# One pair of start addresses for all split weights of the up projection

## The chip, the cores and the metric

The kernel runs on one core of one Trainium2 chip. The metric is the device time of one execution in microseconds (us), and the time of a kernel is the median over several executions.

## The reference, cut to what matters

The program is one layer of a decoder trunk on a sequence of 256 tokens with 2048 channels, all in float32. A token mixer (sparse attention beside a matrix memory) comes first, a channel mixer follows. The change lies in the first matrix product of the channel mixer:

```
def conv_ffn(h, w_up, conv_w, conv_b, w_down):
    a, g = jnp.split(h @ w_up, 2, axis=-1)      # h: 256 x 2048, w_up: 2048 x 11264
    a = causal_dwconv(a, conv_w, conv_b)        # width 3
    return (jax.nn.silu(a) * g) @ w_down        # w_down: 5632 x 2048
```

`h @ w_up` is the "up projection", the product with `w_down` the "down projection".

## The kernel before, in words

**Split operands.** TensorE multiplies here in the format fp32r, which keeps fewer bits than float32. So every operand is split into a high part (rounded) and a low part (what the rounding left), and each product is made of three matmuls: high by high, high by low, low by high. A weight tile `w` of 128 partitions by 1024 float32 numbers (512 KB) comes by one DMA from the SP queue. ScalarE (ACT) casts it to `wh` (line 122), VectorE (DVE) subtracts to get `wl` (line 123). Both go into buffers that are 64 numbers wider than the tile, so that the tile may begin at any of several places in its buffer:

```
wh = wp.tile([P, 1024 + OFFN], F32R, name="wh", tag="wh", bufs=WB[1])[:, off:off + 1024]
wl = wp.tile([P, 1024 + OFFN], F32R, name="wl", tag="wl", bufs=WB[2])
wl = wl[:, offl:offl + 1024]
```

There are four buffers for `wh` and four for `wl`, used in turn. A buffer has (1024 + 64) x 4 = 4352 bytes in each partition, which is 17 x 256, and in the built program each of the eight begins at a multiple of 256 bytes. So the place in the buffer is also the place within 256 bytes: place 16 is byte 64, place 48 is byte 192.

**The up projection.** It is done in 44 blocks, `up(j)` for j = 0 to 43. Each block computes 128 channels of `a` and 128 channels of the gate for all 256 tokens, from four weight tiles of eight 128x128 pieces each. The weights are the stationary operand, and the activations `h2T` (high and low, 256 columns each, already in SBUF, every piece at a multiple of 1024 bytes from a start that is a multiple of 256) are the moving operand. For each piece stand three matmuls of 256 columns (line 93, by way of `mm_b`):

```
mm(ps, a, xt[:, k, 0, :], start, False)     # a: high part of the weights
mm(ps, a, xt[:, k, 1, :], False, False)
mm(ps, b, xt[:, k, 0, :], False, stop)      # b: low part
```

So a block has 4 x 8 x 3 = 96 matmuls, all with a weight load of 128x128 of their own, and writes one PSUM bank, `ps_up`. Afterwards ScalarE and VectorE do convolution, SiLU and gate from that bank while the next block runs.

**The places before.** The table `PLACES` has 22 pairs (place of the high part, place of the low part). Block j of the first half (j = 0 to 21) uses pair j, block j of the second half (22 to 43) uses pair 43 - j. So each pair serves two blocks, in reverse order, and neighbouring blocks nearly always have different pairs.

**What stands around the blocks.** Blocks 0 to 21 come right after the normalisation that makes `h2T` piece by piece; block 0 starts while TensorE still transposes the last pieces (line 1025). From block 3 on, a ticker (`tk.tick`) weaves the loads and products of one more adaptive row (`ada_rows`, lines 186 and 219) into the first half: DVE products, and two groups of eight TensorE transposes called `ps_adar`. Then the first half of the down projection runs (`proj_rows`, tile `ps_d`, 512 columns a matmul at first, 256 columns at the end), then blocks 22 to 43, then the second half of the down projection. Earlier in the program the input projection `ps_b` uses the same three matmuls with weights at one fixed pair of places, (16, 16).

Of the kernel before, what the change touches and what calls it, by code (L numbers as in the profile page):

```python
# [23 lines left out]
KF = DFF // P  # L24
# [14 lines left out]
NU0, NU1 = 4, 1  # L39
WARM = 20  # L40
OFFB, OFFA, OFFN = 16, 48, 64
PLACES = ((16, 16), (0, 0), (8, 8), (24, 24), (32, 32), (40, 40), (48, 48), (56, 56), (16, 16), (4, 4),
          (12, 12), (16, 48), (48, 16), (0, 16), (16, 0), (32, 0), (0, 32), (20, 20), (32, 48), (48, 32),
          (8, 40), (16, 16))
MORD = (0, 2, 1, 3)
PTV = 2
YA = 2
# [10 lines left out]
def build(ctx: ExitStack, tc: tile.TileContext, d, out, dbg=None):  # L58
# [36 lines left out]
    def t2(shape, name, dt=F32):  # L95
        return p0.tile(shape, dt, name=name, tag="t2", bufs=NT2)

    def bank(pool, name, dt=F32):
        return pool.tile([P, 512], dt, name=name, tag="b")

    def load(src):
        n = src.shape[-1]
        t = wp.tile([P, 1024], F32, name="w", tag="w", bufs=WB[0])
        nc.sync.dma_start(t[:, :n], src)
        return t
# [8 lines left out]
    def load_split(src, off=0, offl=None):  # L114

        n = src.shape[-1]
        t = load(src)
        wh = wp.tile([P, 1024 + OFFN], F32R, name="wh", tag="wh", bufs=WB[1])[:, off:off + 1024]
        wl = wp.tile([P, 1024 + OFFN], F32R, name="wl", tag="wl", bufs=WB[2])
        offl = off if offl is None else offl  # L120
        wl = wl[:, offl:offl + 1024]
        nc.scalar.copy(wh[:, :n], t[:, :n])  # L122
        lows.append(nc.vector.tensor_sub(wl[:, :n], t[:, :n], wh[:, :n]))  # L123
        return wh, wl
# [5 lines left out]
    def mm_b(ps, wh, wl, i, xt, k, start, stop):  # L130
        a, b = wh[:, i * P:(i + 1) * P], wl[:, i * P:(i + 1) * P]
        mm(ps, a, xt[:, k, 0, :], start, False)
        mm(ps, a, xt[:, k, 1, :], False, False)
        mm(ps, b, xt[:, k, 0, :], False, stop)
# [375 lines left out]
    for gi, kn in enumerate(GROUPS):  # L510
# [14 lines left out]
        for b in range(NBLK):  # L525
            if b % 2 == 0:
                ps = bank(psm, "ps_b")
            for k in range(k0, k0 + kn):
                wh, wl = next(wb)
# [14 lines left out]
        for c in range(6):  # L544
            pss = [bank(psm, "ps_a%d" % t) for t in range(2)]
            aw = AW if c < 4 else 512
            for k in range(k0, k0 + kn):
                wh, wl = next(wa if c < 4 else wv)
# [542 lines left out]
    KH = KF // 2  # L1091
# [8 lines left out]
    def up(j):  # L1100

        ps = bank(psm, "ps_up")
        for b in range(2):
            for hf in range(2):
                wh, wl = load_split(d["w_up"][j * 4 + b * 2 + hf], *PLACES[j if j < KH else KF - 1 - j])
                for k in range(8):
                    mm_b(ps[:, b * S:(b + 1) * S], wh, wl, k, h2T, hf * 8 + k, hf == 0 and k == 0,
                         hf == 1 and k == 7)
                tk.tick(UR)
        a, gate = ps[:, :S], ps[:, S:]  # L1110
        fw = lambda i: ffn[:, 3 * j + i:3 * j + i + 1]
        av = t2([P, S], "av")
        nc.scalar.activation(av, a, AF.Identity, bias=ffn[:, R_FB + j:R_FB + j + 1], scale=fw(2))
        for i in (1, 0):
            sh = 2 - i
            nc.vector.scalar_tensor_tensor(av[:, sh:], a[:, :S - sh], fw(i), av[:, sh:],
                                           op0=ALU.mult, op1=ALU.add)
        nc.scalar.activation(av, av, AF.Silu)
        nc.vector.tensor_mul(av, av, gate)
        u = uTt[:, j % KH]  # L1120
        nc.scalar.copy(u[:, 0, :], av)
        nc.vector.tensor_sub(u[:, 1, :], av, u[:, 0, :])

    for j in range(KH):
        up(j)
        if j == 2:
            for c in range(2):
                tk.add(ada_rows(5, g2, c))
# [3 lines left out]
    for j in range(KH, KF):  # L1132
        up(j)
# [147 lines left out]
```

## Time and profile before

| what | value |
|---|---|
| median of 3 runs | 1490.48 us |
| lowest and highest run | 1487.12 and 1491.28 us |
| the profiled execution: its time as the profile has it, the span from first to last instruction | 1488.3 us |
| granted TensorE clock, mean over the span | 0.984 |
| TensorE matmuls busy | 1439.8 us, 97% of the span |
| VectorE busy | 1071.9 us, 72% |
| ScalarE busy | 709.8 us, 48% |
| chain that ended last: `ps_up` matmuls | 33% of the span |
| blocks 0 to 21, and 22 to 43, from first to last matmul | 731.8 to 986.3 us, and 1108.1 to 1356.2 us |

The page gives no time of the profiled execution besides its span; the span is 2.2 us below the median of the runs shown. A matmul is recorded from its issue to its modelled end, so neighbours overlap, and the time that one costs is read from the distance of starts, or from a stretch divided by its count. In a view of stretches ("windows") for one tile, the count after PE is of all matmuls that overlap the stretch: a block of 96 shows 96 plus the two or three that are still ending, or beginning, at its edges.

### The profile page before, as it was taken

The page shows a single profiled execution, that of the slowest core. Times are in us where ns is not written, and L with a number is a line of the kernel's source. Part 1 is how long each engine was busy: PE and PEld are TensorE (multiplying, and loading weights), DVE is VectorE, ACT ScalarE, POOL GpSimd, SP SyncE. Part 2 cuts the span into 40 slices and gives each one's busy share as a digit, 9 for nine tenths or more (in the row PEclk, how much of TensorE's full clock was granted, in tenths as well). Part 3 has the DMA queues.
Part 4 walks back from the last instruction along what each step waited for, and adds up shares of the span by engine and source line. Part 5 has one row for each costly group of instructions (what it writes and reads, how often), then busy time and mean ns, then how long its engine had stood idle before and what let it go on. Part 6 is the DMA issues. An engine that isn't in the chain of part 4 may idle for free.

```text
span 1488.3 us, 24079 instructions
## 1 busy us (share of the span) xinstructions
PE 1439.8 (97%) x9470; PEld 1301.9 (87%) x9470; DVE 1071.9 (72%) x1565; ACT 709.8 (48%) x954; POOL 2.1 (0%) x6
## 2 busy tenths in 40 slices
PE   5999999999999999999699999999999999999997
PEld 4998998877667888888599999998899999999886
DVE  7899887888677898689867767755555555555566
ACT  5654443637664444435554444443334444444341
POOL 0000000000000000000000000000000000000000
PEclk8999999999999999999899999999999999999998
DMA  9999897885767999999078878866665555655661
GB/s 359 346 351 353 312 325 265 314 317 181 269 236 273 329 316 324 331 343 335 28 251 277 287 232 282 275 196 195 193 203 187 184 186 191 189 185 186 196 210 59
DMA packets 104081, 374.81 MB, mean 252 GB/s; under 512 B 11680, under 2 KB 12192, under 8 KB 103200
## 3 DMA queue, kind: packets, MB, share of 16 engines
q1 hardware_dynamic: 103968, 373.27, 72.9%
q8 instruction: 74, 1.21, 0.3%
q14 instruction: 39, 0.32, 0.1%
HBM read 371.13 MB, written 2.10 MB: 251 GB/s over the span
## 4 chain that ended last, share of the span: by engine, by line
PE 86%; DVE 7%; ACT 2%; DMA 2%; issue 2%; SPq 0%; DVEq 0%; ACTq 0%
PE ps_up L93 33%; PE ps_d L93 16%; PE ps_mg L93 11%; PE ps_b L93 7%; PE ps_br L93 6%; PE ps_o L93 5%; PE ps_a L93 5%; DVE w L186 2%; DVE wl L123 2%; DMA w<-in_w_in_b_dram 1%; PE ps_y L93 1%; ACT wh L122 1%; DVE xz L955 1%; DVE xz L960 1%; PE ps_hid L93 1%
## 5 line engine op out<-in xcount | busy, mean ns | idle before, releaser
L123 DVE TENSOR_TENSOR wl<-w,wh 128x1024 fp32r<-128x1024 f32 (+1 forms) x478 | 575.9, 1205 | 352.3 <-ACT wh L122 350.6
L122 ACT CAST wh<-w 128x1024 fp32r<-128x1024 f32 (+1 forms) x478 | 495.5, 1038 | 659.2 <-PE ps_up L93 205.5
L93 PE MATMUL ps_up<-h2T,wh 128*128 128x256 f32 x2816 | 499.3, 281 | 0.5 <-DVE h2T L1082 0.3
L93 PEld LDWEIGHTS ps_up<-h2T,wh 128*128 128x128 f32 x2816 | 431.4, 189 | 1.3 <-DVE h2T L1082 0.7
L93 PE MATMUL ps_up<-h2T,wl 128*128 128x256 f32 x1408 | 394.6, 280 | 0.0
L93 PEld LDWEIGHTS ps_up<-h2T,wl 128*128 128x128 f32 x1408 | 265.8, 189 | 0.1
L186 DVE SCALAR_TENSOR_TENSOR w<-w,crow 128x1024 f32<-128x1024 f32 x192 | 233.3, 1217 | 1.4 <-DMA w<-in_w_ada_dram 1.4
L93 PE MATMUL ps_d<-wh,uTt 128*128 128x512 f32 (+1 forms) x792 | 209.8, 353 | 0.0
L93 PE MATMUL ps_mg<-wh,hT 128*128 128x512 f32 x512 | 171.6, 406 | 0.0
L93 PEld LDWEIGHTS ps_d<-wh,uTt 128*128 128x128 f32 x792 | 139.7, 188 | 20.7
L93 PE MATMUL ps_d<-wl,uTt 128*128 128x512 f32 (+1 forms) x396 | 139.8, 353 | 0.0
L93 PE MATMUL ps_b<-hT,wh 128*128 128x256 f32 x768 | 134.6, 280 | 3.1 <-ACT wh L122 3.1
L93 PEld LDWEIGHTS ps_b<-hT,wh 128*128 128x128 f32 x768 | 116.7, 189 | 7.8 <-issue 3.7
L93 PEld LDWEIGHTS ps_mg<-wh,hT 128*128 128x128 f32 x512 | 97.1, 190 | 24.2 <-issue 4.4
L93 PE MATMUL ps_a<-wh,hT 128*128 128x392 f32 (+1 forms) x384 | 110.5, 363 | 1.8 <-ACT wh L122 1.8
L93 PE MATMUL ps_b<-hT,wl 128*128 128x256 f32 x384 | 105.6, 280 | 0.6 <-DVE wl L123 0.5
L93 PE MATMUL ps_mg<-wl,hT 128*128 128x512 f32 x256 | 100.6, 393 | 0.0
L93 PEld LDWEIGHTS ps_d<-wl,uTt 128*128 128x128 f32 x396 | 74.4, 188 | 10.2
L93 PEld LDWEIGHTS ps_a<-wh,hT 128*128 128x128 f32 x384 | 71.5, 190 | 10.4 <-ACT wh L122 2.8
L93 PEld LDWEIGHTS ps_b<-hT,wl 128*128 128x128 f32 x384 | 72.2, 190 | 1.4 <-DVE wl L123 1.0
L93 PE MATMUL ps_a<-wl,hT 128*128 128x392 f32 (+1 forms) x192 | 70.0, 364 | 1.0 <-DVE wl L123 1.0
L93 PE MATMUL ps_o<-wh,mgT 128*128 128x512 f32 (+1 forms) x224 | 64.9, 374 | 0.0
(252 smaller groups left out, 1218.8 us busy)
## 6 DMA issues: line engine op xcount, KB each, us to landing
w<-in_w_ada_dram SPq DMA_DIRECT2D x192, 512.0 KB, 5.0
w<-in_w_up_dram SPq DMA_DIRECT2D x176, 512.0 KB, 4.3
w<-in_w_down_dram SPq DMA_DIRECT2D x90, 512.0 KB, 4.2
w<-in_w_mg_dram SPq DMA_DIRECT2D x64, 512.0 KB, 5.1
w<-in_w_in_b_dram SPq DMA_DIRECT2D x48, 512.0 KB, 5.3
w<-in_w_br_dram SPq DMA_DIRECT2D x32, 512.0 KB, 5.5
w<-in_w_o_dram SPq DMA_DIRECT2D x32, 512.0 KB, 5.0
w<-in_w_in_a_dram SPq DMA_DIRECT2D x32, 392.0 KB, 4.3
```

The costliest lines, as they stand in the source:

```text
L93: nc.tensor.matmul(o, lhsT, rhs, start=start, stop=stop)
L122: nc.scalar.copy(wh[:, :n], t[:, :n])
L123: lows.append(nc.vector.tensor_sub(wl[:, :n], t[:, :n], wh[:, :n]))
L186: ins = nc.vector.scalar_tensor_tensor(t, t, 1.0, crow[:, i * 1024:(i + 1) * 1024], op0=ALU.mult, op1=ALU.mult, accum_out=parts[:, row(m), ...
L955: nc.vector.scalar_tensor_tensor(z, z, mv[:, 0:1], lg[:, c * 512:(c + 1) * 512], op0=ALU.subtract, op1=ALU.mult)
L960: nc.vector.scalar_tensor_tensor(z, z, mv[:, 2:3], lb[:, c * 512:(c + 1) * 512], op0=ALU.mult, op1=ALU.add, accum_out=acc)
```

## The change

All 44 blocks of the up projection take the pair (16, 48): the high part begins at byte 64 of its buffer, the low part at byte 192. The table goes away, and with it the dependence on j. On every engine the built program has the same instructions in the same order as before; what differs are the start addresses in the casts, the subtractions and the weight loads of these blocks. Blocks 11 and 32 have this pair already; the other 42 change.

```
-PLACES = ((16, 16), (0, 0), (8, 8), (24, 24), (32, 32), (40, 40), (48, 48), (56, 56), (16, 16), (4, 4),
-          (12, 12), (16, 48), (48, 16), (0, 16), (16, 0), (32, 0), (0, 32), (20, 20), (32, 48), (48, 32),
-          (8, 40), (16, 16))
+PLACE = (16, 48)
...
-                wh, wl = load_split(d["w_up"][j * 4 + b * 2 + hf], *PLACES[j if j < KH else KF - 1 - j])
+                wh, wl = load_split(d["w_up"][j * 4 + b * 2 + hf], *PLACE)
```

## The prediction

> **What bounds the kernel now.** I read the page first: the engine shares, the slices, and the chain that ended last.
>
> ```profile
> PE 1439.8 (97%) x9470; PEld 1301.9 (87%) x9470; DVE 1071.9 (72%) x1565; ACT 709.8 (48%) x954; POOL 2.1 (0%) x6
> ...
> PE   5999999999999999999699999999999999999997
> ...
> PE 86%; DVE 7%; ACT 2%; DMA 2%; issue 2%; SPq 0%; DVEq 0%; ACTq 0%
> PE ps_up L93 33%; PE ps_d L93 16%; PE ps_mg L93 11%; PE ps_b L93 7%; PE ps_br L93 6%; PE ps_o L93 5%; PE ps_a L93 5%; DVE w L186 2%; DVE wl L123 2%; DMA w<-in_w_in_b_dram 1%; PE ps_y L93 1%; ACT wh L122 1%; DVE xz L955 1%; DVE xz L960 1%; PE ps_hid L93 1%
> ```
>
> TensorE is busy in nearly every slice, it is 86% of the chain, and the matmuls of the up projection alone are a third. So each nanosecond in the pace of these 4224 matmuls counts, if nothing else takes over the bound. Next, therefore, the stretches that the blocks fill, all engines (columns: stretch, its length, busy time of PE, weight loads, DVE, ACT, POOL, granted clock, DMA share, GB/s), and the wait of the casts:
>
> ```profile
> 748.53:872.72 124.19, 124.19 (x1058) 124.19 (x1057) 89.40 (x122) 60.11 (x78) 0.00 (x0) 1.00 0.77 262
> 1108.10:1356.24 248.14, 248.14 (x2115) 248.14 (x2114) 142.21 (x176) 115.14 (x151) 0.00 (x0) 1.00 0.60 189
> ...
> ACT wh L122 <- PE ps_up L93: 205.5, 134, 1.8
> ```
>
> Both stretches are PE without a gap at the full granted clock. In the tighter one (blocks 1 to 11) DVE is busy 89.40 of 124.19 us and DMA at 0.77; ACT waits for PE to free its buffers, not the reverse. Work for a PE that is 4% faster is thus at hand: DVE would go from 72% to 75% there and DMA from 0.77 to 0.80.
>
> Then the same view for `ps_up` alone, one stretch per block from its first matmul to the next block's first. This is where the change is to be read, because the table before is a trial of 22 pairs of places, each seen twice.
>
> ```profile
> core 0: us, PE busy (x) PEld busy (x) DVE busy (x) ACT busy (x), PEclk, DMA share, GB/s
> 748.53:760.00 11.47, 11.47 (x99) 11.47 (x97) 1.38 (x3) 0.56 (x1) 1.00 0.72 264
> ...
> 805.66:816.96 11.30, 11.30 (x98) 11.30 (x97) 1.37 (x3) 0.56 (x1) 1.00 0.82 282
> ...
> 828.27:839.17 10.90, 10.90 (x99) 10.90 (x97) 1.37 (x3) 0.56 (x1) 1.00 0.81 288
> ...
> 861.84:872.72 10.88, 10.88 (x98) 10.88 (x97) 1.38 (x3) 0.55 (x1) 1.00 0.66 211
> 872.72:878.05 5.33, 5.33 (x50) 5.33 (x48) 0.96 (x2) 0.56 (x1) 1.00 0.61 195
> 879.16:884.74 5.58, 5.58 (x49) 5.58 (x48) 0.20 (x1) 0.00 (x0) 1.00 0.76 272
> ...
> 975.44:986.34 10.90, 10.90 (x98) 10.87 (x96) 1.37 (x3) 0.56 (x1) 1.00 0.62 194
> 1108.10:1119.41 11.31, 11.31 (x96) 11.31 (x97) 0.00 (x0) 0.00 (x0) 1.00 0.70 217
> ...
> 1209.90:1221.32 11.42, 11.42 (x99) 11.42 (x98) 1.37 (x3) 0.56 (x1) 1.00 0.58 186
> 1221.32:1232.23 10.91, 10.91 (x99) 10.91 (x97) 1.37 (x3) 0.56 (x1) 1.00 0.60 193
> ...
> 1254.90:1266.20 11.30, 11.30 (x98) 11.30 (x97) 1.37 (x3) 0.56 (x1) 1.00 0.57 187
> ...
> 1277.40:1288.29 10.89, 10.89 (x98) 10.89 (x97) 1.37 (x3) 0.56 (x1) 1.00 0.60 194
> ...
> 1333.82:1345.34 11.52, 11.52 (x99) 11.52 (x97) 1.37 (x3) 0.56 (x1) 1.00 0.58 182
> 1345.34:1356.24 10.90, 10.90 (x98) 10.86 (x96) 1.37 (x3) 0.56 (x1) 1.00 0.60 193
> ```
>
> The rows in order are blocks 1 (0, 0); 6 (48, 48); 8 (16, 16); 11 (16, 48); 12 (48, 16) in two parts, with a break between; 21 and 22 (16, 16); 31 (48, 16); 32 (16, 48); 35 (16, 16); 37 (48, 48); 42 (0, 0); 43 (16, 16). The reader is to see three things. The same 96 matmuls take 10.88 to 11.52 us, and the second visit of (0, 0) is as slow as the first, so places matter. The pair of the change, (16, 48), took 10.88 and 10.91, the fastest there is: 113.3 ns a matmul. But the place is not all: (16, 16) took 10.90 in blocks 8, 21 and 43 and 11.30 in 22 and 35, and (48, 48) took 11.30 and then 10.89. With places 16 and 48, a stream has (at least) two paces, 113.3 and 117.8 ns, and stays in the one that it came into.
>
> **Which pace a stream comes into.** Two entries and the input projection, which runs at (16, 16) throughout, show that. PE by time first:
>
> ```profile
> 877.82 0.39 PE L93 MATMUL ps_up<-h2T,wh 128*128 128x256 f32 x2
> ...
> 878.16 1.03 PE L219 MATMUL ps_adar<-cst,modc 128*128 128x128 f32 x8
> 878.95 0.48 PE L93 MATMUL ps_up<-h2T,wh 128*128 128x256 f32 x2
> ...
> 1107.98 0.28 PE L93 MATMUL ps_d<-wh,uTt 128*128 128x256 f32 x1
> 1108.10 0.40 PE L93 MATMUL ps_up<-h2T,wh 128*128 128x256 f32 x2
> ```
>
> Block 12 was fast (5.33 us for its first 47 steps), eight transposes broke in, and its rest ran slow (5.58). Block 22 follows the 256-column end of the down projection without a gap, which ran at the slow pace, and block 22 kept it. The input projection's stretches (tile `ps_b`):
>
> ```profile
> 83.39:111.80 28.41, 28.41 (x252) 28.41 (x251) 6.84 (x10) 0.00 (x0) 1.00 0.95 343
> 112.21:114.70 2.49, 2.49 (x22) 2.49 (x22) 0.68 (x1) 0.00 (x0) 1.00 0.96 334
> ...
> 151.00:187.00 36.00, 35.91 (x317) 35.71 (x315) 7.51 (x11) 0.00 (x0) 1.00 0.87 313
> 221.75:229.00 7.25, 7.25 (x62) 7.25 (x62) 0.69 (x1) 0.00 (x0) 1.00 0.55 192
> ```
>
> With unchanging places the pace holds: about 113 ns over 252 and over 317 matmuls, 117 over the 62 that follow wide matmuls. So after the change the 44 blocks are three streams: block 0 (once `h2T` is complete) to the break in block 12; from there to block 21; blocks 22 to 43. Each takes one pace at its start.
>
> **The change part by part.** *Order and counts*: nothing is removed, added or moved on any engine or queue; cost zero. *Casts and subtractions*: the DVE count and busy time in the block rows above are the epilogue's; the 176 subtractions change only their target's place, and are hidden while DVE has a quarter of each stretch free; I take zero, with that slack as the cover. *The breaks for other work* (block 12's transposes, block 0's start): they stay. *Pace of the weight loads and matmuls*: this is the whole sum. The stretches, again for `ps_up`:
>
> ```profile
> 740.99:748.53 7.54, 7.54 (x63) 7.54 (x64) 0.00 (x0) 0.00 (x0) 1.00 0.87 307
> 748.53:872.72 124.19, 124.19 (x1058) 124.19 (x1057) 15.11 (x33) 6.13 (x11) 1.00 0.77 262
> 879.16:884.74 5.58, 5.58 (x49) 5.58 (x48) 0.20 (x1) 0.00 (x0) 1.00 0.76 272
> 884.74:986.34 101.60, 101.60 (x866) 101.57 (x864) 12.35 (x27) 5.04 (x9) 1.00 0.78 264
> 1108.10:1356.24 248.14, 248.14 (x2112) 248.10 (x2112) 28.80 (x63) 11.74 (x21) 1.00 0.60 189
> ```
>
> At block 11's 10.88 us: tail of block 0, 63 x 113.3 ns = 7.14, saves 0.40. Blocks 1 to 11: 11 x 10.88 = 119.68, saves 4.51. Rest of block 12, 47 x 113.3 ns = 5.33, saves 0.25. Blocks 13 to 21: 9 x 10.88 = 97.92, saves 3.68. Blocks 22 to 43: 22 x 10.88 = 239.36, saves 8.78. Sum 17.6 us, by stream 4.9, 3.9 and 8.8. The profiled span of 1488.3 would become 1470.7; the median lies 2.2 above the span, so 1490.5 - 17.6 = 1472.9, rounded to 1473. This is the end of the bounds on the good side. The other end is the slowest pace seen with places 16 and 48, block 31's 11.42 us at (48, 16): 11 x 11.42 = 125.62 (+1.43), 102.78 (+1.18), 251.24 (+3.10), together +5.7 with what block 12's first half loses set aside.
>
> I take the fast end for the point, as the likeliest single outcome, because (16, 48) came into the fast pace both times that it was tried, each time out of a slower stream: at block 11 from 11.31, and at block 32 straight out of the slow form of (48, 16), at 11.42. Every other pair of 16s and 48s has been seen slow at least once. That is two entries, both at a change of place, and none at a break, which is why the chance stays under a half.
>
> [...]
>
> **The rivals.** *The slow stream is kept* (no change). For it: block 22 took over the slow pace of the down projection with no gap, the transposes left block 12 slow, and block 0's tail ran slow at (16, 16), so all three streams would start where a slow one was seen. At 11.31 us a block the stretches give +0.22, +0.19 and +0.68, with 0.2 for block 12's first half +1.3: 1491.8. Against it: block 32. *Some streams fast, some slow*: the third alone fast saves 8.8 less 0.6, so 1482.3; the first two alone save 8.8 less 0.7, so 1482.4; first and third 13.7 less 0.2, so 1477; the first alone 4.9 less 0.9, so 1486.5. *The slow form of unequal places* (slower): if (16, 48) has the slow pace that (48, 16) showed, and the streams come into it at block 0, at the transposes and after the down projection, all of them lose: 1490.5 + 5.7 = 1496.2. It decides from about 11.40 us a block in all three, since 42 x 0.1 us is then what is lost against today's mean of about 11.3. Against it again is block 32, which left just that form. *The place has no effect and the pace is luck of the entry*: against it are the repeats at (0, 0); it would give 1482 to 1492 and goes with the mixed case.
>
> **How the numbers follow.** All fast 0.46, at 1470 to 1476 (the runs before spread over 4.2 us). Mixed 0.26, at 1477 to 1487, of which about 0.05 end within 4.5 us of the median before. Slow stream kept 0.19, at 1490 to 1493. Slow form of unequal places 0.09, at 1494 to 1497. A measurement of this kernel can tell about 0.3%, 4.5 us. So faster 0.46 + 0.21 = 0.67, within 0.3% 0.05 + 0.19 and a little of the last case, 0.26, slower 0.07. The range 1470 to 1492.5 takes in all but the last case and some edges.
>
> **What would show it.** In the profile after, block starts 10.88 us apart from block 1 on, and 2112 matmuls of the second half in 239.4 us, show the sum right; 11.31 or 11.42 in a whole stream shows the entry to have decided against it. Steps at the eight transposes, and block 22's first matmuls against the down projection's last, show whether a break changes the pace. It is wrong in another way if PE shows idle time before `ps_up` (casts, subtractions or DMA too late for a faster PE), or if the down projection's pace moves with that of the blocks ahead of it.

## The result and the profile after

The changed kernel takes 1472.96 us (median of 4 runs, 1472.32 to 1477.86) against 1490.12 us for the kernel before, measured beside it; the ratio is 0.9895, 95% interval 0.9877 to 0.9912. So it is faster, by 17.2 us or 1.15% by the medians. The ratio goes by the means of the runs, in which the longest run weighs more; there it is 15.6 us, 1.05%. A second measurement, further down, gave 1471.83 us and 0.9870 (0.9853 to 0.9886).

The span of the profiled execution is 1475.8 us. From its page, the engines and the chain that ended last (line numbers are two lower than before, since the table is gone):

```profile
PE 1427.3 (97%) x9470; PEld 1289.4 (87%) x9470; DVE 1072.2 (73%) x1565; ACT 710.7 (48%) x954; POOL 2.1 (0%) x6
...
PE ps_up L91 32%; PE ps_d L91 16%; PE ps_mg L91 11%; PE ps_b L91 8%; PE ps_br L91 6%; PE ps_o L91 5%; PE ps_a L91 5%; DMA w<-in_w_in_v_dram 1%; DVE w L184 1%; DVE wl L121 1%; PE ps_y L91 1%; ACT wh L120 1%; DVE xz L953 1%; DVE xz L958 1%; DMA w<-in_w_in_b_dram 1%
```

TensorE still sets the time: PE is 88% of the chain that ended last, by the page. It is busy for 12.5 us less, and VectorE and ScalarE are unchanged within 1 us. Then the stretches of the up projection, all `ps_up`, columns as before: block 0's tail, block 1, blocks 1 to 11, the rest of block 12, blocks 13 to 21, block 22, blocks 22 to 43.

```profile
746.01:753.27 7.26, 7.26 (x64) 7.26 (x64) 0.00 (x0) 0.00 (x0) 1.00 0.83 269
753.27:764.15 10.88, 10.88 (x99) 10.88 (x97) 1.38 (x3) 0.56 (x1) 1.00 0.86 311
...
753.27:872.95 119.68, 119.68 (x1059) 119.68 (x1057) 15.15 (x33) 6.13 (x11) 1.00 0.80 274
879.39:884.72 5.33, 5.33 (x49) 5.33 (x49) 0.20 (x1) 0.00 (x0) 1.00 0.81 291
884.72:982.63 97.91, 97.91 (x866) 97.88 (x864) 12.39 (x27) 5.01 (x9) 1.00 0.81 274
1104.40:1115.31 10.91, 10.91 (x97) 10.91 (x97) 0.00 (x0) 0.00 (x0) 1.00 0.69 220
1104.40:1343.78 239.38, 239.38 (x2112) 239.35 (x2112) 28.88 (x63) 11.72 (x21) 1.00 0.64 196
```

All three streams run at 113.3 ns a matmul: 119.68 us for 124.19 before, 97.91 for 101.60, 239.38 for 248.14. Together that is 16.96 us, and 0.54 us more came in block 0's tail (7.26 us for 7.55, which the prediction's row gives as 7.54) and in the rest of block 12 (5.33 for 5.58). The most telling row is block 22: it begins with no gap behind the slow end of the down projection, as before, and takes 10.91 us where it took 11.31. That end, the 256-column part of `ps_d`, took 30.98 us for 263 matmuls before, 117.8 ns each, and runs at 117.8 ns in the changed kernel too; the row of before:

```profile
1077.12:1108.10 30.98, 30.98 (x265) 30.94 (x263) 2.14 (x5) 1.00 0.62 193
```

The timeline of PE shows how:

```profile
1104.28 0.28 PE L91 MATMUL ps_d<-wh,uTt 128*128 128x256 f32 x1
1104.40 0.40 PE L91 MATMUL ps_up<-h2T,wh 128*128 128x256 f32 x2
1104.64 0.28 PE L91 MATMUL ps_up<-h2T,wl 128*128 128x256 f32 x1
1104.76 0.40 PE L91 MATMUL ps_up<-h2T,wh 128*128 128x256 f32 x2
1104.99 0.28 PE L91 MATMUL ps_up<-h2T,wl 128*128 128x256 f32 x1
1105.11 0.39 PE L91 MATMUL ps_up<-h2T,wh 128*128 128x256 f32 x2
1105.34 0.28 PE L91 MATMUL ps_up<-h2T,wl 128*128 128x256 f32 x1
1105.45 0.39 PE L91 MATMUL ps_up<-h2T,wh 128*128 128x256 f32 x2
1105.67 0.28 PE L91 MATMUL ps_up<-h2T,wl 128*128 128x256 f32 x1
1105.79 0.39 PE L91 MATMUL ps_up<-h2T,wh 128*128 128x256 f32 x2
```

Three matmuls take 0.36 us at first (1104.40 to 1104.76) and 0.34 from 1105.11 on: the stream arrives slow and is fast after about six matmuls. The eight transposes in block 12 no longer leave it slow either: its rest takes 113.4 ns a matmul (5.33 us for 47).

The profiled execution is some 5 us longer than the other three (1477.86 us against 1472.32 to 1473.11). Its block 1 begins at 753.27 us, that of the kernel before at 748.53. The delay arises where no place was changed, between 290 and 310 us: the same matmul of `ps_a` begins at 289.96 us, before at 290.06, and the first of `ps_mg` at 308.57, before at 303.61. First the row of before, then of after, all engines:

```profile
290.00:310.00 20.00, 20.00 (x105) 16.60 (x105) 17.94 (x34) 9.57 (x13) 0.00 (x0) 0.91 0.78 253
```

```profile
290.00:310.00 20.00, 18.78 (x83) 15.44 (x82) 16.13 (x30) 11.38 (x14) 0.00 (x0) 0.74 0.72 243
```

The granted clock was 0.74 instead of 0.91 there, and 83 matmuls were done instead of 105. By an estimate from these two rows, 0.17 of 20 us is 3.4 us of clock, and 1.2 us of idle time (18.78 us busy of 20) came on top. Why less clock was granted in this execution, no run here shows.

### The profile page after: what moved, and what is told of

The parts are those of the page before. It is cut to its first block, busy times and chain, and to the rows that moved or that the text cites. A ratio compares the mean times of both kernels' runs of the same rounds, so it can differ in the third digit from the quotient of the medians.

```text
span 1475.8 us, 24079 instructions
## 1 busy us (share of the span) xinstructions
PE 1427.3 (97%) x9470; PEld 1289.4 (87%) x9470; DVE 1072.2 (73%) x1565; ACT 710.7 (48%) x954; POOL 2.1 (0%) x6
## 4 chain that ended last, share of the span: by engine, by line
PE 88%; DVE 6%; DMA 3%; ACT 2%; issue 1%; SPq 0%; DVEq 0%; ACTq 0%
PE ps_up L91 32%; PE ps_d L91 16%; PE ps_mg L91 11%; PE ps_b L91 8%; PE ps_br L91 6%; PE ps_o L91 5%; PE ps_a L91 5%; DMA w<-in_w_in_v_dram 1%; DVE w L184 1%; DVE wl L121 1%; PE ps_y L91 1%; ACT wh L120 1%; DVE xz L953 1%; DVE xz L958 1%; DMA w<-in_w_in_b_dram 1%
## 5 line engine op out<-in xcount | busy, mean ns | idle before, releaser
L120 ACT CAST wh<-w 128x1024 fp32r<-128x1024 f32 (+1 forms) x478 | 496.0, 1039 | 646.1 <-PE ps_up L91 191.9
L91 PE MATMUL ps_up<-h2T,wh 128*128 128x256 f32 x2816 | 481.9, 277 | 0.5 <-DVE h2T L1080 0.3
L91 PEld LDWEIGHTS ps_up<-h2T,wh 128*128 128x128 f32 x2816 | 424.9, 188 | 1.2 <-DVE h2T L1080 0.7
L91 PE MATMUL ps_up<-h2T,wl 128*128 128x256 f32 x1408 | 389.0, 276 | 0.0
```

The source lines that it names most:

```text
L91: nc.tensor.matmul(o, lhsT, rhs, start=start, stop=stop)
```

## The experiments

Three theories about the pace of a stream were put against each other. "Pair": the pair (16, 48) has no lasting slow pace, others have one. "Unbroken": any pair of 16s and 48s is fast once the places no longer change. "Luck": streams come in fast or slow at random.

**All blocks at (16, 16).**

```
-PLACE = (16, 48)
+PLACE = (16, 16)
```

> All 44 blocks at the pair (16, 16): unchanging places as in the changed kernel, but another pair. Theory 'pair' ((16, 48) has no lasting slow pace, other pairs have one, so that what a stream comes in with stays): blocks 22 to 43 take over the down projection's 117.8 ns and keep it, 11.31 us a block; block 0's tail and the blocks after the eight transposes were seen slow at (16, 16) or (48, 16), so all three streams slow: 1490 to 1492 us, and at best one stream fast (1482 to 1487). Rival 'unbroken' (any pair of 16s and 48s is fast once the places no longer change from block to block): 10.88 us a block, 1473. Rival 'luck' (entries fall at random): between, and different from run to run.

Measured: 1487.32 us over 10 runs (1484.63 to 1491.09), ratio 0.9978 (0.9965 to 0.9990). Its `ps_up` stretches, blocks 1 to 11, 13 to 21, 22 to 43:

```profile
746.65:866.33 119.68, 119.68 (x1058) 119.68 (x1057) 15.14 (x33) 6.15 (x11) 1.00 0.80 275
878.30:979.94 101.64, 101.64 (x865) 101.64 (x864) 12.38 (x27) 5.06 (x9) 1.00 0.79 264
1101.81:1350.56 248.75, 248.75 (x2112) 248.70 (x2112) 28.86 (x63) 11.80 (x21) 1.00 0.61 188
```

The first stream is fast up to the transposes, the second slow (11.3 us a block), and the third keeps the down projection's slow pace for all 2112 matmuls. "Unbroken" falls. Once in, each stream at (16, 16) kept its pace here: on average 113.3 ns over 1056 matmuls, 117.6 over 864, 117.8 over 2112.

At the start of block 0, though, the entry at (16, 16) is not fixed. The kernel before has the same pair in block 0, behind the same work, and its last 63 steps there took 7.54 us (the prediction's row); here they take 7.26:

```profile
739.39:746.65 7.26, 7.26 (x63) 7.26 (x64) 0.00 (x0) 0.00 (x0) 1.00 0.81 256
```

So "luck" is not ruled out for (16, 16). The profile is that of the shortest of the ten runs, 1484.63 us; whether the first stream was fast in the longer ones too is not shown.

**All blocks at (48, 16).**

```
-PLACE = (16, 48)
+PLACE = (48, 16)
```

> All 44 blocks at (48, 16), the same two places with high and low part exchanged. Theory 'pair': the slow form of blocks 12 and 31 lasts, 11.42 us a block in all three streams, 1496 us; at least the third stream slow. Rival 'unbroken': 1473. A third idea, that only the difference of 128 bytes between high and low part counts, also says 1473.

Measured: 1476.8 us (1475.08 to 1478.12), ratio 0.9903 (0.9885 to 0.9921). The same three stretches:

```profile
746.92:866.60 119.68, 119.68 (x1058) 119.68 (x1057) 15.12 (x33) 6.13 (x11) 1.00 0.81 275
878.62:981.34 102.72, 102.72 (x866) 102.67 (x864) 12.38 (x27) 5.02 (x9) 1.00 0.78 261
1103.08:1342.48 239.40, 239.40 (x2112) 239.35 (x2112) 28.84 (x63) 11.71 (x21) 1.00 0.64 196
```

My expectation of 1496 was wrong: only the stream after the transposes is slow, at 11.41 us a block. The third turned fast behind the slow down projection, which (16, 16) did not. So the exchanged pair does have the slow form that blocks 12 and 31 showed, but it did not stay in it behind the down projection. The third idea of the expectation, that only the difference of 128 bytes counts, falls with the slow second stream.

**Only the second half at (16, 48).** The edit is to the kernel before, and its table stays.

```
-                wh, wl = load_split(d["w_up"][j * 4 + b * 2 + hf], *PLACES[j if j < KH else KF - 1 - j])
+                wh, wl = load_split(d["w_up"][j * 4 + b * 2 + hf], *(PLACES[j] if j < KH else (16, 48)))
```

> Only blocks 22 to 43 at (16, 48), blocks 0 to 21 with the table of before. Theory 'pair': block 22 takes a few slow matmuls from the down projection and then 113.3 ns, blocks 23 to 43 10.88 us each; saves 8.8 us of 1490.1, 1481.3. 'luck': block 22 may stay at 117.8, then 22 x 11.31 us, no gain, 1491.

Measured: 1480.73 us (1479.68 to 1483.23), ratio 0.9932 (0.9915 to 0.9949). Blocks 1 to 11, block 22, blocks 22 to 43:

```profile
748.46:872.64 124.18, 124.18 (x1058) 124.18 (x1057) 15.14 (x33) 6.14 (x11) 1.00 0.78 263
1108.03:1118.94 10.91, 10.91 (x97) 10.91 (x97) 0.00 (x0) 0.00 (x0) 1.00 0.71 217
1108.03:1347.42 239.39, 239.39 (x2112) 239.35 (x2112) 28.87 (x63) 11.69 (x21) 1.00 0.64 196
```

The first half keeps its 124.18 us, the second takes 239.39: 9.7 us by the medians (8.75 by the stretch). The gain is where it was summed.

**The weights' address or their distance from the moving operand?** Three kernels move `h2T` itself; the second argument of `big` is where it begins in its buffer, in numbers of 4 bytes. In the first the weights stay at (16, 48).

```
-    h2T = big("h2T")
+    h2T = big("h2T", 16)
```

> The changed kernel with the moving operand h2T begun 64 bytes later; weights stay at (16, 48). Theory 'distance' (what counts is where the weights begin against the moving operand, within 256 bytes): the distances are now those of the pair (0, 32), which took 11.44 us a block before, so 119 ns a matmul in all blocks and 17.6 us lost plus a little: 1496 to 1498 us. Rival 'absolute' (the weights' own address counts): 113.3 ns, 1473.

Measured: 1497.38 us (1494.26 to 1499.15), ratio 1.0045 (1.0031 to 1.0059), slower than the kernel before.

```
-PLACE = (16, 48)
+PLACE = (32, 0)
...
-    h2T = big("h2T")
+    h2T = big("h2T", 16)
```

> h2T begun 64 bytes later and the weights at (32, 0) in all 44 blocks. 'distance': high part 64 bytes behind h2T, low part 64 before, which within 256 bytes is the pair (16, 48): 113.3 ns everywhere, after the transposes and after the down projection too, 1473 us. 'absolute': (32, 0) took 11.36 us a block twice: 118.3 ns, 1492.

Measured: 1471.8 us (1469.63 to 1474.59), ratio 0.9876 (0.9858 to 0.9894).

```
-PLACE = (16, 48)
+PLACE = (48, 16)
...
-    h2T = big("h2T")
+    h2T = big("h2T", 32)
```

> h2T begun 128 bytes later and all blocks at (48, 16). 'distance' within 256 bytes: it is (16, 48) again, fast in all three streams, the one after the transposes too, 1473 us. 'distance' within 128 bytes, or 'absolute': as with (48, 16) and h2T unmoved, 118.9 ns in blocks 12 to 21, 1477 us.

Measured: 1474.97 us (1472.88 to 1476.67), ratio 0.9892 (0.9873 to 0.9910). The stretches of blocks 1 to 11, 13 to 21 and 22 to 43, one fence for each of the three kernels in this order:

```profile
746.78:872.56 125.78, 125.78 (x1059) 125.78 (x1058) 15.12 (x33) 6.16 (x11) 1.00 0.77 257
884.86:987.77 102.91, 102.91 (x866) 102.87 (x864) 12.37 (x27) 5.03 (x9) 1.00 0.77 261
1109.53:1361.09 251.56, 251.56 (x2112) 251.51 (x2112) 28.79 (x63) 11.74 (x21) 1.00 0.60 186
```

```profile
748.54:868.22 119.68, 119.68 (x1059) 119.68 (x1057) 15.12 (x33) 6.14 (x11) 1.00 0.81 274
880.01:977.93 97.92, 97.92 (x866) 97.89 (x864) 12.36 (x27) 5.01 (x9) 1.00 0.82 274
1099.68:1339.05 239.37, 239.37 (x2112) 239.34 (x2112) 28.84 (x63) 11.69 (x21) 1.00 0.64 196
```

```profile
752.10:871.78 119.68, 119.68 (x1058) 119.68 (x1057) 15.12 (x33) 6.13 (x11) 1.00 0.82 273
883.55:981.47 97.92, 97.92 (x866) 97.88 (x864) 12.37 (x27) 5.01 (x9) 1.00 0.81 275
1103.23:1342.63 239.40, 239.40 (x2112) 239.36 (x2112) 28.82 (x63) 11.70 (x21) 1.00 0.64 196
```

With the same weight places and `h2T` 64 bytes later, a block takes 11.43 us (251.56 / 22), which is what the pair (0, 32) took before, in blocks 16 and 27:

```profile
918.71:930.16 11.45, 11.45 (x99) 11.45 (x98) 1.37 (x3) 0.56 (x1) 1.00 0.79 274
...
1164.50:1175.93 11.43, 11.43 (x98) 11.43 (x97) 1.38 (x3) 0.56 (x1) 1.00 0.56 185
```

With the places moved along, all is fast again (10.88 us a block). With `h2T` at 128 bytes, (48, 16) is fast after the transposes as well (97.92 us), where it had been slow (102.72). So in these kernels the distance between weights and moving operand within 256 bytes decides, not the weights' own address; within 128 bytes is not enough.

One more cause can be set aside from the traces: that the casts and subtractions, which write at the same places, hold up the reads. In the second half of the kernel with (16, 16) everywhere, a step takes 117.8 ns on average, both where a cast or a subtraction is writing into its buffer meanwhile (1828 steps) and where none is (283 steps).

**The input projection too.** The changed kernel, with `w_in_b` at (16, 48) instead of (16, 16).

```
-    def stream(src, width, per, off=0):
+    def stream(src, width, per, off=0, offl=None):
...
-            wh, wl = load_split(src[next(tiles)][:, :width * per], off)
+            wh, wl = load_split(src[next(tiles)][:, :width * per], off, offl)
...
-    wb, wa, wv = (stream(d[n], w, p, o) for n, w, p, o in (("w_in_b", P, 8, OFFB), ("w_in_a", AW, 2, 0),
-                                                           ("w_in_v", 512, 2, 0)))
+    wb, wa, wv = (stream(d[n], w, p, *o) for n, w, p, o in (("w_in_b", P, 8, PLACE), ("w_in_a", AW, 2, (0,)),
+                                                           ("w_in_v", 512, 2, (0,))))
```

> The changed kernel, and the input projection's weights (tile ps_b) at (16, 48) as well instead of (16, 16). In the profile of the changed kernel 6 stretches of ps_b with 663 matmuls ran at 117.8 ns, in that of the kernel before only 133 did; 530 x 4.4 ns = 2.4 us, about half of the 4.9 us by which the profiled run of the changed kernel is above its other three. Theory 'pair': no lasting 117.8 in ps_b; all runs at 1470 to 1473, none near 1478. Rival: the input projection waits for DMA (share 0.95), so the pace of ps_b changes nothing and a run near 1478 can still occur.

Measured: 1469.88 us (1469.62 to 1471.93), ratio 0.9860 (0.9845 to 0.9875). To see it beside the changed kernel, both ran again on one chip:

> The changed kernel once more, as the base for the next two on the same chip: 1472 to 1474 us, with single runs up to 1478 where the input projection comes in slow.

> Up and input projection at (16, 48) once more: 1470 us, 2 to 3 us below the changed kernel of this call, if the input projection's pace is what it gains; 1473 if the first result was the chip's.

Measured there: the changed kernel 1471.83 us (1469.79 to 1473.6), ratio 0.9870 (0.9853 to 0.9886); with the input projection 1470.94 us (1469.99 to 1475.76), ratio 0.9870 (0.9853 to 0.9887). One stretch of `ps_b`, of the changed kernel and then of the other, in these last runs:

```profile
147.66:183.00 35.34, 35.34 (x302) 35.34 (x302) 7.33 (x11) 0.00 (x0) 1.00 0.87 301
```

```profile
151.07:186.41 35.34, 35.34 (x313) 35.34 (x313) 7.53 (x11) 0.00 (x0) 1.00 0.88 310
```

The pace changes as foreseen, 113 for 117 ns, but the gain of about a microsecond is less than the 2 to 3 us expected and not clear of the spread. My expectation put half of the long profiled run down to the pace of `ps_b`; that was wrong. The changed kernel's profile here has the slow `ps_b` and took only 1471.35 us, and the run at 1475.76 us is without it. What does go with the length of a run is the granted clock between 290 and 310 us, here for the changed kernel and then for the other:

```profile
290.00:310.00 20.00, 20.00 (x102) 16.93 (x102) 18.09 (x34) 9.02 (x11) 0.00 (x0) 0.91 0.84 266
```

```profile
290.00:310.00 20.00, 19.35 (x94) 15.66 (x93) 16.59 (x31) 11.30 (x15) 0.00 (x0) 0.83 0.73 248
```

It does so in all eight profiles of kernels whose blocks are all at the fast distances: the four runs of 1475.76 to 1477.86 us have a granted clock of 0.74 or 0.83 there, the four of 1471.09 to 1473.13 us have 0.91 or 1.00.

**The down projection.** There the weights move and the activations are stationary. The line is that of a helper, which serves the 256-column end of the output projection (`ps_o`) too. On top of the kernel with the input projection:

```
-                    wh, wl = load_split(w[base + n], OFFA)
+                    wh, wl = load_split(w[base + n], 48, 16)
```

> The input projection at (16, 48), and the 256-column part of the down projection too, where the weights move and the activations are the stationary operand: its weights at (48, 16), so that the stationary operand stands at the distances (16, 48). Twice 264 matmuls ran at 117.8 ns there; of these, 264 and 132 have the new places (the others read held tiles at (48, 48)). 'distance': 113.3 ns for those, 396 x 4.4 ns = 1.8 us below the kernel with the input projection alone (1469.9): 1468.1. Rival (weights matter only as the stationary operand): 117.8 stays, 1469.9.

and, in another kernel, with `16, 48` in that line:

> The same and the 256-column part of both down projections and of the output projection at (16, 48) in place of (48, 16); weights move there. In the kernel with (48, 16) all of that part ran at 117.8 ns. If the order of the two distances is what matters: 113.3 ns for 396 matmuls of ps_d, 1.8 us below the kernel with the input projection alone. If the moving form has its slow pace at unequal places too: no gain, and the output projection's end (192 matmuls, fast at (48, 48)) may lose 0.9 us.

Measured: 1474.07 us (1471.09 to 1481.25), ratio 0.9893 (0.9873 to 0.9913), and 1474.21 us (1470.92 to 1476.14), ratio 0.9883 (0.9868 to 0.9898). The 256-column end of the first down projection, `ps_d`, with (48, 16) and then with (16, 48):

```profile
1066.53:1097.51 30.98, 30.98 (x265) 30.98 (x263) 2.22 (x5) 1.00 0.62 191
```

```profile
1072.08:1102.98 30.90, 30.90 (x265) 30.85 (x263) 2.25 (x5) 1.00 0.65 195
```

Neither is fast. The first stretch is 263 steps, 117.8 ns each, the second 264, 117.0 ns each; at 113.3 ns they would take 29.8 and 29.9 us. The output projection's end, `ps_o`, lost by it: in 20.23 us it did 180 matmuls at (48, 48), in the changed kernel, 173 at (48, 16) and 178 at (16, 48).

```profile
699.78:720.01 20.23, 20.23 (x180) 20.22 (x179) 2.55 (x5) 1.00 0.66 250
```

```profile
691.77:712.00 20.23, 20.23 (x173) 20.23 (x172) 2.52 (x5) 1.00 0.62 243
```

```profile
698.37:718.60 20.23, 20.23 (x178) 20.23 (x177) 2.54 (x5) 1.00 0.66 250
```

So the rule of distances, as I had worded it, does not carry over to the form in which the places of the moving operand alternate. What would make that form fast was not found, and neither kernel is better than the one with the input projection alone.

## Why the prediction was right, point by point

- *The bound.* TensorE was the bound and stayed it; with DVE at 0.75 of the first stream and DMA at 0.80 nothing else was late. The wait of the casts for `ps_up` only shrank, from 205.5 to 191.9 us. Blocks 1 to 11, all engines, and that wait:

```profile
753.27:872.95 119.68, 119.68 (x1059) 119.68 (x1057) 89.20 (x122) 60.30 (x78) 0.00 (x0) 1.00 0.80 274
...
ACT wh L120 <- PE ps_up L91: 191.9, 135, 1.7
```

- *The sum.* Foreseen were 119.68, 97.92 and 239.36 us for the three stretches; measured were 119.68, 97.91 and 239.38. Foreseen in all were 17.6 us; the stretches give 17.5, the medians 17.2. The one term that was off is block 0's tail, 7.26 us for 7.14: the first of its 63 steps, next to the last transposes of `h2T`, takes 0.23 us (0.22 before), and the sum had it at 0.113.
- *The point.* The median foreseen from the 2.2 us above the span was 1473; it is 1472.96. The agreement to a tenth is luck, since single runs differ by 5 us. The step from span to time is sound: every run on record lies 2.0 to 2.1 us above its own span.
- *Order, casts, breaks.* No cost appeared, as said: VectorE's busy time is 1072.2 us for 1071.9.
- *"Each takes one pace at its start".* This step failed for (16, 48). It held at (16, 16), in the kernel with that pair everywhere (113.3, 117.6 and 117.8 ns). At (16, 48), or at the same distances with `h2T` moved, no entry that occurs in these kernels left a lasting slow stream: not the start of block 0, not the transposes, not the slow down projection. That is 25 streams in nine profiles, all fast (the stretches of ten of them, in four profiles, stand above, at 113.3 to 113.4 ns); streams that come in at random would hardly do that. I had read the two fast visits as two draws; they were the rule, and block 32, which left a slow stream of (48, 16), was the row that said so.
- *The rivals.* "The slow stream is kept" happens, but at (16, 16) (1487.32 us, with one stream fast). "The slow form of unequal places" exists, but at (48, 16), and in the kernel with that pair everywhere only after the transposes (1476.8 us). "Place has no effect" fell with the moved `h2T`.
- *The place.* The measurement decides that it matters: moving `h2T` by 64 bytes against unmoved weights costs 25 us (1497.38 against 1472 to 1473), so the pace does depend on where the two operands stand against each other. Which part of the chip makes it so, no run here shows.

## What to carry to other kernels

Where a stream of 256-column matmuls loads new weights for each, look at the distance of starts, not at busy time: here 113.3 or 117 to 120 ns, with PE 100% busy in both. Try where the operands begin within 256 bytes, and judge a place by whether it turns a slow stream fast (its behaviour after a break, and right behind a slow neighbour), not only by its best stretch; (16, 16) had as good a best stretch as (16, 48), 119.68 us for blocks 1 to 11. Keep the distance, not the address: when either operand's buffer moves, the other has to follow; here 64 bytes cost 25 us. All this was shown for split weights as the stationary operand; with the split weights moving, as in the down projection, these distances did not help (117.8 and 117.0 ns).

## What the runs showed of the hardware that I had not expected

- For three matmuls with weights high, high, low against one moving operand, distances of 64 and 192 bytes gave 113.3 ns from every entry seen (25 streams). Equal distances of 64 have two lasting paces, 113.3 and 117.8 ns, and one of them held for 2112 matmuls on end. 192 and 64 have 113.3 and 118.9; 0 and 128 run at 119 (11.43 us a block).
- A slow pace passed without a gap from one matrix product to the next: from the end of the down projection (117.8 ns in the kernel before) into block 22 at (16, 16) there (11.31 us), and into all 22 blocks of the kernel with that pair everywhere (248.75 us, 117.8 ns).
- A granted clock of 0.74 instead of 0.91 over 20 us, with 1.2 us of idle time, 430 us ahead of the changed part, went with a delay of one run by some 5 us (308.57 for 303.61 us at the first `ps_mg`), nearly a third of what the change gives. A comparison of single runs, or of two profiled spans (12.5 us here), would have mis-sized it.
